# Attention of one transformer block: low value products one block later, merged steps, other filler rates

## The chip, the cores and the metric

The kernel runs on one core of one Trainium2 chip. The metric is the device time of one execution in microseconds, the median of several runs. Matrix products run on TensorE (PE in the profile, its weight loads PEld), elementwise work on VectorE (DVE), ScalarE (ACT) and GpSimd (POOL), and transfers are issued by SyncE (SP).

## What is computed

One transformer block over 512 positions with a model width of 1024, in float32. Cut to what matters here:

```python
proj = rmsnorm(x) @ w_in                       # queries, keys, values, gates
o_nsa = nsa_attention(...)                     # 8 heads, 2 key groups: compressed + selected + window
o_swa = swa_attention(...)                     # 8 heads, 2 key groups: window of 128, a sink per head
x = x + rmsnorm(concat([o_nsa, o_swa]) @ w_o)
x = x + rmsnorm((gelu(conv(h @ w_gate)) * (h @ w_up)) @ w_down)   # h = rmsnorm(x), 2816 wide
x = x + (p @ w_ple) * sigmoid(x @ w_ple_gate)
# inside each attention, per query block: s = q k^T * scale - slope * distance, masked;
# p = softmax(s) (SWA: with the sink in the denominator); o = p v
```

## The kernel before

Every float32 operand of a product is split into a high and a low part, and a product is three matmuls (high by high, low by high, high by low; `mm3`, L129) of up to 512 columns. The stages come in order: load and normalise, value projection, compressed keys, the first query projections, the attention, output projection, feed-forward, gate.

The attention goes by 16 units, a unit being one key group and one block of 128 queries (in the order 3, 0, 2, 1): eight NSA units (two groups), then eight SWA units. A unit has two parts, each a Python generator that issues a step's instructions and then yields a number of nanoseconds:

- Scores. `nsa_scores` (L592) has two steps a head, eight in all: score matmuls, bias and minimum on VectorE (L611), exponentials on ScalarE (L615), scaling by gate over sum on GpSimd (L521). `swa_scores` (L551) has four steps with the scores of a head each (L565, L567), and a fifth with the small operations, the exponentials (L578) and the scaling (L584).
- Value products. `pv` (L523) goes over the key blocks of a unit: four transposes of the probabilities into PSUM (L499), a copy of the high part on ScalarE (L501), the low part by subtraction on VectorE (L503), then two matmuls into one PSUM bank: the high product (L533) and the low product (L534). They come one block behind the transposes. After the last block `put_out` (L506) copies the sum out (L510, L515, L517, L518). The split tiles have three slots, the scores three PSUM banks, the transposes two and the sum one.

`together` (L664) merges the score steps of a unit with the product steps of the unit before it, so that both advance by equal fractions. After each step `fill` (L157) adds the step's nanoseconds times a rate (`RATES`, L55, for NSA group 0, 1, SWA group 0, 1) to a credit, and while the credit is positive it takes 650 off and issues one filler step. Fillers are work from elsewhere: the query and key projections that later units need (tiles 3, 8, 4, 5, 6, 7 in this order; nine steps each, eight of them one `mm3`), and, appended once unit 8's steps are out, the first half of the output projection (`out_proj_first`, L767; 33 steps, 32 of them three matmuls, L762 to L764), which reads the finished NSA outputs. What a unit needs is finished by `drain` ahead of it. What is left at the end is issued after the last unit.

The order on each engine is made by the compiler: it simulates the program with a time model and gives an engine the earliest instruction in program order that is ready. A filler's first matmul is also tied (`pin`, L139) behind an attention matmul, `self.last`, the last one issued before it; `att` (L178) keeps that. After the attention, `out_proj` (L780) computes the second half, and its matmuls of the later SWA group (`mixmm`, L757) need the last unit's output.

Of the kernel before, what the change touches and what calls it, by code (L numbers as in the profile page):

```python
# [14 lines left out]
P = 128  # L15
# [36 lines left out]

FILL_STEP = 650.0
WARM = 9
RATES = [0.5, 0.5, 0.7, 0.7]  # L55


class Block:
    def __init__(self, tc, io, ctx):
        self.tc = tc  # L60
        self.nc = tc.nc
        self.io = io
        en = ctx.enter_context
        self.cp = en(tc.tile_pool(name="const", bufs=1))
        self.up = en(tc.tile_pool(name="u", bufs=1))
        self.wrp = en(tc.tile_pool(name="wr", bufs=2))
        self.rp = en(tc.tile_pool(name="rb", bufs=2))
        self.sp = en(tc.tile_pool(name="s", bufs=4))
        self.tp = en(tc.tile_pool(name="tiny", bufs=2))
        self.pp = en(tc.tile_pool(name="ps", bufs=1, space=bass.MemoryType.PSUM))  # L70
        self.n = 0
        self.ordered = False
        self.e = []
        self.phase = "x"
        self.mark = {}
        self.fillers = []
        self.credit = 0.0
        self.rate = 1.0
        self.last = None
        self.pinned = None  # L80

    @contextmanager
# [74 lines left out]
    def fill(self, ns):  # L157

        self.credit += ns * self.rate
        while self.credit > 0 and self.fillers:  # L160
            self.credit -= FILL_STEP
            self.fill_step()

    def fill_step(self):
        phase, self.phase = self.phase, "fill"
        self.pinned = self.last
        try:
            next(self.fillers[0])
        except StopIteration:
            self.fillers.pop(0)  # L170
        self.pinned = None
        self.phase = phase
# [3 lines left out]
            self.fill_step()  # L176

    def att(self, r):  # L178
        self.last = r.ins
        return r  # L180


# [340 lines left out]
    def pv(self, blocks, mix, qt):  # L523

        nc = self.nc
        po = self.ps("o")
        n = len(blocks)

        def product(i, t, rows, v):
            if rows < P:  # L530
                self.att(nc.tensor.matmul(po, v, t[: 2 * rows, 0, :], start=i == 0, stop=i == n - 1))
                return
            self.att(nc.tensor.matmul(po, v, t[:, 0, :], start=i == 0, stop=False))  # L533
            self.att(nc.tensor.matmul(po, v, t[:, 1, :], start=False, stop=i == n - 1))  # L534

        late = None
        for i, (srcs, rows, v) in enumerate(blocks):
            t = self.transpose_split(srcs, rows)
            if late is not None:
                product(*late)  # L540
            late = (i, t, rows, v)
            yield 602
        product(*late)
        self.put_out(po, mix, qt)
        yield 1000

# [4 lines left out]
    def swa_scores(self, u):  # L551
        self.phase = "swa"
        nc = self.nc
        g, qt = u["g"], u["qt"]
        kh, kl = self.ks
        n = P if qt == 0 else 2 * P
        k0 = 0 if qt == 0 else (qt - 1) * P
        b0 = P if qt == 0 else 0
        p = self.u([P, 4, 2 * P], F32, "p")
        nm = self.tiny([P, 4], "nm")  # L560
        for r in range(4):
            if r % 2 == 0:
                ps = self.ps("s")
            o = ps[:, r % 2 * 256 : r % 2 * 256 + 256]
            self.score(ps, o, self.q[4 + 2 * g + r // 2][:, r % 2, qt * P : (qt + 1) * P],  # L565
                       kh[:, g, k0 : k0 + 256], kl[:, g, k0 : k0 + 256])
            nc.vector.tensor_tensor_reduce(p[:, r, :n], o[:, :n], self.dist_w[:, b0:], op0=ALU.add, op1=ALU.min,  # L567
                                           scale=SLOPES[4 * g + r], scalar=3e38, accum_out=nm[:, r : r + 1])
            yield 70 + n
        ns = self.nsink[:, 4 * g : 4 * g + 4]  # L570
        nm2 = self.tiny([P, 4], "nm2")
        nc.vector.tensor_tensor(nm2, nm, ns, op=ALU.min)
        es = self.tiny([P, 4], "es")
        nc.vector.tensor_sub(es, nm2, ns)
        nc.scalar.activation(es, es, AF.Exp)
        sm = self.tiny([P, 4], "sm")
        for r in range(4):
            nc.scalar.activation(p[:, r, :n], p[:, r, :n], AF.Exp, bias=nm2[:, r : r + 1], scale=-1.0,  # L578
                                 accum_out=sm[:, r : r + 1])
        rc = self.tiny([P, 4], "rc")  # L580
        nc.vector.tensor_add(rc, sm, es)
        nc.vector.reciprocal(rc, rc)
        for r in range(4):
            self.scale_rows(p[:, r, :n], rc[:, r : r + 1])  # L584
        yield 400
        u["blocks"] = [
            ([p[:, r, b * P : (b + 1) * P] for r in range(4)], P,
             self.vs[k0 // P + b][:, 4 + g].rearrange("p a d -> p (a d)"))
            for b in range(n // P)
        ]  # L590
# [70 lines left out]
    def mix_tiles(self):  # L661
        return [self.u([P, 2, T], F32R) for _ in range(2)]

    def together(self, a, b):  # L664

        gens = [(x, n) for x, n in (a, b) if x is not None]
        done = [0] * len(gens)
        alive = [True] * len(gens)
        while any(alive):
            k = min((k for k in range(len(gens)) if alive[k]), key=lambda k: (done[k] + 1) / gens[k][1])  # L670
            try:
                ns = next(gens[k][0])
                done[k] += 1
                self.fill(ns)
            except StopIteration:
                alive[k] = False

    def attention(self):
        io = self.io
# [2 lines left out]
        mix = [None] * 4  # L682
# [44 lines left out]
        units += [dict(kind="s", g=g, qt=qt) for g in range(2) for qt in (3, 0, 2, 1)]  # L727
        before = None
        for i, u in enumerate(units + [None]):
            sc = None  # L730
            if u is not None:
                k = u["g"] + (0 if u["kind"] == "n" else 2)
                need = [[], [2, 3], [8, 4, 5], [6, 7]][k]
                for f in need:
                    if f in qf:
                        self.drain(qf[f])
                if mix[k] is None:
                    mix[k] = self.mix_tiles()
                self.rate = RATES[k]
                u["mix"] = mix[k]  # L740
                sc = (self.nsa_scores(u), 8) if u["kind"] == "n" else (self.swa_scores(u), 5)
            bp = None
            if before is not None:
                bp = (self.pv(before["blocks"], before["mix"], before["qt"]), len(before["blocks"]) + 1)
            self.together(sc or (None, 1), bp or (None, 1))
            if i == NQT * 2:
                self.mix = []
                for k in range(2):
                    self.mix += [(mix[k][0][:, i, :], mix[k][1][:, i, :]) for i in range(2)]
                self.fillers.append(self.out_proj_first())  # L750
            before = u
# [264 lines left out]
```

## Time and profile before

| | us |
|---|---|
| three runs | 690.43, 691.87, 692.05 |
| their median | 691.87 |
| the profiled execution, device time | 691.2 |
| its span, first to last instruction | 689.4 |
| TensorE busy in the span | 665.5 |

The profile is one execution. A busy matmul row says little of how close together matmuls start, since each one's modelled end lies past the start of the next. The attention runs from about 75 to 236 us of the span.

### The profile page before, as it was taken

Reading aid. Unit: us, or ns where it says so; the run is one execution under the profiler, and the core shown is the slowest. Engines: PE = TensorE matmul, PEld = TensorE weight load, DVE = VectorE, ACT = ScalarE, POOL = GpSimd, SP = SyncE. Lnnn points to the kernel's source line nnn. Section 1 sums busy time; section 2 is a strip of 40 time slices with the busy share of each in tenths; the row PEclk is TensorE's granted clock in tenths of the full one; section 3 lists DMA queues with packets and bytes.
Section 4 is the critical chain, followed back from the end, with each engine's and each line's share of the span. In section 5 each row is a group of like instructions: output and inputs, shape, how many; then the busy total and the mean of one; then the engine's idle time right before and its main releaser. Section 6 shows DMA issues by size and latency. Waiting matters only on the chain.

```text
span 689.4 us, 8840 instructions
## 1 busy us (share of the span) xinstructions
PE 665.5 (97%) x3111; PEld 545.1 (79%) x3111; DVE 399.9 (58%) x808; ACT 324.9 (47%) x603; POOL 170.4 (25%) x235
## 2 busy tenths in 40 slices
PE   8999999999979897999999999999999999999996
PEld 7988777887758685888888888888888888887785
DVE  6786767767964468767555455554542232325853
ACT  7453758867796455445333343333432222233341
POOL 1112658757375152422010110101100000100000
PEclk9999999999999999999999999999999999999999
DMA  8537523111106143042233322233323323344032
GB/s 290 178 99 222 145 62 78 46 47 48 47 1 214 38 162 121 15 140 92 92 101 109 97 91 92 92 99 116 92 85 86 105 85 101 97 145 152 2 106 77
DMA packets 25116, 70.05 MB, mean 102 GB/s; under 512 B 3184, under 2 KB 4464, under 8 KB 25072
## 3 DMA queue, kind: packets, MB, share of 16 engines
q1 hardware_dynamic: 24928, 69.42, 32.1%
q8 instruction: 24, 0.39, 0.2%
q14 instruction: 20, 0.16, 0.1%
q10 hardware_dynamic: 144, 0.08, 0.0%
HBM read 60.05 MB, written 2.10 MB: 90 GB/s over the span
## 4 chain that ended last, share of the span: by engine, by line
PE 87%; DVE 5%; ACT 5%; DMA 1%; issue 1%; POOL 0%; ACTq 0%; DVEq 0%
PE mlpup_pss L136 4%; PE mlpup_pss L137 4%; PE mlpup_pss L133 4%; PE mlpup_psmm L136 3%; PE mlpup_psmm L133 3%; PE mlpup_psmm L137 3%; PE mlpup_pst L136 3%; PE mlpup_pst L137 3%; PE mlpup_pst L133 3%; PE nsa_pst L499 3%; PE mlpdown_pss L133 2%; PE mlpdown_pss L137 2%; PE mlpdown_pss L136 2%; ACT swa_u L578 2%; PE fill_psmm L133 2%; PE fill_psmm L136 2%
## 5 line engine op out<-in xcount | busy, mean ns | idle before, releaser
L117 ACT ACTIVATE mlpup_wh<-mlpup_wr 128x1024 fp32r<-128x1024 f32 x40 | 42.3, 1060 | 83.3 <-PE mlpup_pss L136 27.7
L870 POOL TENSOR_TENSOR mlpup_s<-mlpup_s,r3b 128x512 f32<-128x512 f32 x22 | 29.3, 1332 | 188.0 <-ACT mlpup_s L869 188.0
L117 ACT ACTIVATE mlpdown_wh<-mlpdown_wr 128x1024 fp32r<-128x1024 f32 (+1 forms) x24 | 23.7, 989 | 84.7 <-PE mlpdown_pss L136 33.9
L121 DVE TENSOR_TENSOR mlpdown_wh<-mlpdown_wr,mlpdown_wh 128x1024 fp32r<-128x1024 f32 (+1 forms) x24 | 27.3, 1136 | 62.2 <-ACT mlpdown_wh L117 62.2
L121 DVE TENSOR_TENSOR mlpup_wh<-mlpup_wr,mlpup_wh 128x1024 fp32r<-128x1024 f32 x40 | 49.4, 1236 | 10.6 <-ACT mlpup_wh L117 10.5
L136 PE MATMUL mlpup_pss<-r_u,mlpup_wh 128*128 128x512 f32 x120 | 46.8, 390 | 0.2 <-DVE mlpup_wh L121 0.2
L133 PE MATMUL mlpup_pss<-r_u,mlpup_wh 128*128 128x512 f32 x120 | 46.8, 390 | 0.0
L137 PE MATMUL mlpup_pss<-r_u,mlpup_wh 128*128 128x512 f32 x120 | 46.7, 389 | 0.0
L521 POOL TENSOR_SCALAR nsa_u<-nsa_u,nsa_nrc,gate 128x512 f32<-128x512 f32 (+3 forms) x64 | 38.3, 609 | 26.8 <-DVE nsa_nrc L646 19.2
L615 ACT ACTIVATE nsa_u<-nsa_u,nsa_nnm 128x512 f32<-128x512 f32 (+3 forms) x64 | 35.4, 555 | 7.1 <-DVE nsa_nnm L611 6.5
L503 DVE TENSOR_TENSOR nsa_u<-nsa_pst,nsa_u 128x512 fp32r<-128x512 f32 (+1 forms) x44 | 30.0, 688 | 14.9 <-ACT nsa_u L501 14.6
L611 DVE CUSTOM_DVE_ANT_0 nsa_u<-nsa_pss,biastables_u 128x512 f32<-128x512 f32 (+3 forms) x64 | 30.2, 486 | 6.6 <-PE nsa_pss L549 6.4
L501 ACT ACTIVATE nsa_u<-nsa_pst 128x512 fp32r<-128x512 f32 (+1 forms) x44 | 25.5, 589 | 15.8 <-PE nsa_pst L499 15.6
L221 POOL TENSOR_TENSOR mlpdown_s<-mlpdown_s,mlpdown_s 128x512 f32<-128x512 f32 x6 | 7.8, 1296 | 100.2 <-ACT mlpdown_s L220 100.2
L869 ACT ACTIVATE mlpup_s<-mlpup_s 128x512 f32<-128x512 f32 x22 | 13.8, 631 | 38.6 <-DVE mlpup_s L868 38.6
L121 POOL TENSOR_TENSOR fill_wh<-fill_wr,fill_wh 128x512 fp32r<-128x512 f32 (+1 forms) x14 | 24.7, 1761 | 28.7 <-ACT fill_wh L117 28.7
L133 PE MATMUL mlpup_pst<-r_u,mlpup_wh 128*128 128x512 f32 x80 | 31.2, 390 | 0.0
L137 PE MATMUL mlpup_pst<-r_u,mlpup_wh 128*128 128x512 f32 x80 | 31.1, 389 | 0.0
L136 PE MATMUL mlpup_pst<-r_u,mlpup_wh 128*128 128x512 f32 x80 | 31.1, 389 | 0.0
L133 PE MATMUL mlpup_psmm<-r_u,mlpup_wh 128*128 128x512 f32 x80 | 31.1, 389 | 0.0
L136 PE MATMUL mlpup_psmm<-r_u,mlpup_wh 128*128 128x512 f32 x80 | 31.1, 389 | 0.0
L137 PE MATMUL mlpup_psmm<-r_u,mlpup_wh 128*128 128x512 f32 x80 | 31.1, 389 | 0.0
(396 smaller groups left out, 1941.7 us busy)
## 6 DMA issues: line engine op xcount, KB each, us to landing
mlpup_wr<-in_gu_dram SPq DMA_DIRECT2D x40, 512.0 KB, 3.3
mlpdown_wr<-in_down_dram SPq DMA_DIRECT2D x16, 512.0 KB, 3.6
fill_wr<-in_win_dram SPq DMA_DIRECT2D x6, 512.0 KB, 3.5
mlpdown_wr<-in_down_dram SPq DMA_DIRECT2D x8, 384.0 KB, 3.2
fill_u<-fill_u SPq DMA_DIRECT2D x20, 128.0 KB, 2.3
loadx_u<-in_xT_dram SPq DMA_DIRECT2D x8, 256.0 KB, 4.8
compress_u<-projk_u SPq DMA_DIRECT2D x16, 128.0 KB, 2.3
fill_wr<-in_wo_dram SPq DMA_DIRECT2D x8, 256.0 KB, 3.0
```

The lines of the kernel that those rows point to most:

```text
L117: nc.scalar.activation(hi, raw, AF.Copy)
L121: eng.tensor_sub(lw, raw, hi.bitcast(F32))
L133: r = self.pin(mm(ps, hi, x[:, 0, :], start=start, stop=False))
L136: mm(ps, lo, x[:, 0, :], start=False, stop=False)
L137: mm(ps, hi, x[:, 1, :], start=False, stop=stop)
L499: self.att(nc.tensor.transpose(pt[:rows, r * P : (r + 1) * P], src, self.ident))
L501: nc.scalar.activation(t[:rows, 0, :], pt[:rows], AF.Copy)
L503: nc.vector.tensor_sub(lo, pt[:rows], t[:rows, 0, :].bitcast(F32))
L521: self.nc.gpsimd.tensor_scalar(ap, ap, col, gate, op0=ALU.mult, op1=ALU.mult)
L611: nc.vector.tensor_tensor_reduce(dst, src, dist, op0=ALU.add, op1=ALU.min, scale=SLOPES[8 + 4 * g + r], scalar=3e38, accum_out=nm[:, r, b ...
L615: nc.scalar.activation(dst, dst, AF.Exp, bias=nm[:, r, b : b + 1], scale=-1.0, accum_out=sm[:, r, b : b + 1])
L870: nc.gpsimd.tensor_mul(c0, c0, self.r3)
```

## The change

Four edits. In `pv` the high product still comes one block behind the transposes, and the low product now two blocks behind. `together` takes a list of keys for each generator, one for each step, and always advances the generator whose next key is least: NSA scores have (j + 1) / 8, products 0.2 + (j + 1) / n, and SWA scores four zeros and a 2.0, so that an SWA unit's first four steps come first, then the products of the unit before it, then the step with the exponentials. A filler is tied to the last attention matmul of six steps back (`LAG`) in place of the last one. The rates go from 0.5, 0.5, 0.7, 0.7 to 0.36, 0.36, 0.9, 0.6, and SWA score steps yield 100, 100, 100 and 4 n + 380 in place of 70 + n each.

```diff
-RATES = [0.5, 0.5, 0.7, 0.7]
+RATES = [0.36, 0.36, 0.9, 0.6]
+LAG = 6
...
-        self.last = None
+        self.steps = [None]
...
         self.credit += ns * self.rate
+        self.steps.append(self.steps[-1])
         while self.credit > 0 and self.fillers:
...
-        self.pinned = self.last
+        self.pinned = self.steps[max(0, len(self.steps) - 1 - LAG)]
...
     def att(self, r):
-        self.last = r.ins
+        self.steps[-1] = r.ins
         return r
...
-        def product(i, t, rows, v):
-            if rows < P:
-                self.att(nc.tensor.matmul(po, v, t[: 2 * rows, 0, :], start=i == 0, stop=i == n - 1))
-                return
-            self.att(nc.tensor.matmul(po, v, t[:, 0, :], start=i == 0, stop=False))
-            self.att(nc.tensor.matmul(po, v, t[:, 1, :], start=False, stop=i == n - 1))
-
-        late = None
+        def product(i, part, start, stop):
+            t, rows, v = ts[i]
+            rhs = t[: 2 * rows, 0, :] if rows < P else t[:, part, :]
+            self.att(nc.tensor.matmul(po, v, rhs, start=start, stop=stop))
+
+        ts = []
         for i, (srcs, rows, v) in enumerate(blocks):
-            t = self.transpose_split(srcs, rows)
-            if late is not None:
-                product(*late)
-            late = (i, t, rows, v)
+            ts.append((self.transpose_split(srcs, rows), rows, v))
+            if i > 0:
+                product(i - 1, 0, i == 1, False)
+            if i > 1:
+                product(i - 2, 1, False, False)
             yield 602
-        product(*late)
+        last = blocks[-1][1] == P
+        product(n - 1, 0, n == 1, False)
+        if n > 1:
+            product(n - 2, 1, False, not last)
+        if last:
+            product(n - 1, 1, False, True)
         self.put_out(po, mix, qt)
         yield 1000
...
-            yield 70 + n
+            yield 100 if r < 3 else 4 * n + 380
...
-    def together(self, a, b):
-
-        gens = [(x, n) for x, n in (a, b) if x is not None]
-        done = [0] * len(gens)
-        alive = [True] * len(gens)
-        while any(alive):
-            k = min((k for k in range(len(gens)) if alive[k]), key=lambda k: (done[k] + 1) / gens[k][1])
+    def together(self, *gens):
+
+        left = [(g, list(keys)) for g, keys in gens]
+        while left:
+            k = min(range(len(left)), key=lambda k: left[k][1][0] if left[k][1] else 0.0)
             try:
-                ns = next(gens[k][0])
-                done[k] += 1
+                ns = next(left[k][0])
+                left[k][1].pop(0)
                 self.fill(ns)
             except StopIteration:
-                alive[k] = False
+                left.pop(k)
...
-                sc = (self.nsa_scores(u), 8) if u["kind"] == "n" else (self.swa_scores(u), 5)
-            bp = None
+                if u["kind"] == "n":
+                    gens.append((self.nsa_scores(u), [(j + 1) / 8 for j in range(8)]))
+                else:
+                    gens.append((self.swa_scores(u), [0.0, 0.0, 0.0, 0.0, 2.0]))
             if before is not None:
-                bp = (self.pv(before["blocks"], before["mix"], before["qt"]), len(before["blocks"]) + 1)
-            self.together(sc or (None, 1), bp or (None, 1))
+                n = len(before["blocks"]) + 1
+                gens.append((self.pv(before["blocks"], before["mix"], before["qt"]), [0.2 + (j + 1) / n for j in range(n)]))
+            self.together(*gens)
```

## Rows read from the trace of the kernel before

**Rows 1.** The page: span, and busy time, share and instructions by engine.
```profile
span 689.4 us, 8840 instructions
...
PE 665.5 (97%) x3111; PEld 545.1 (79%) x3111; DVE 399.9 (58%) x808; ACT 324.9 (47%) x603; POOL 170.4 (25%) x235
```

**Rows 2.** Windows by stage: stretch, its length, busy us by engine, granted clock, DMA.
```profile
76.00:181.00 105.00, 103.24 (x567) 83.00 (x566) 77.52 (x305) 77.44 (x212) 68.73 (x110) 1.00 0.25 65
181.00:205.00 24.00, 19.56 (x112) 15.07 (x111) 19.56 (x93) 21.99 (x81) 14.23 (x32) 1.00 0.01 2
205.00:234.00 29.00, 27.84 (x134) 22.33 (x132) 13.12 (x24) 18.41 (x36) 12.55 (x15) 1.00 0.43 145
234.00:242.00 8.00, 6.09 (x18) 4.55 (x19) 3.41 (x6) 3.32 (x6) 0.81 (x2) 0.79 0.10 33
310.00:600.00 290.00, 290.00 (x1279) 239.78 (x1278) 136.62 (x161) 99.49 (x120) 31.36 (x24) 1.00 0.31 95
```

**Rows 3.** TensorE's waits, 76 to 250 us: who waits for whom, total, times, longest.
```profile
PE outproj_psmm L762 <- ACT swa_u L517: 2.1, 1, 2.1
PE swa_pso L533 <- DVE swa_s L515: 1.6, 2, 0.9
...
PE fill_psmm L762 <- ACT fill_u L778: 1.0, 1, 1.0
PE nsa_pso L534 <- DVE nsa_u L503: 0.9, 4, 0.2
PE fill_psmm L763 <- POOL nsa_u L518: 0.9, 1, 0.9
```

**Rows 4.** Windows of the filler matmuls alone: stretch, length, TensorE's busy us, clock, DMA.
```profile
76.00:181.00 105.00, 42.01 (x150) 1.00 0.25 65
181.00:198.00 17.00, 0.00 (x0) 1.00 0.01 2
...
205.00:234.00 29.00, 17.68 (x72) 1.00 0.43 145
```

**Rows 5.** The chain of waits, 181 to 205 us: shares by engine and line.
```profile
by line: ACT swa_u L578 40.0%; ACT swa_u L501 10.7%; DVE swa_u L567 7.7%; DVE swa_u L503 7.6%; issue 6.9%; DVE nsa_s L515 3.5%; DVE swa_nm L572 3.1%; ACT swa_s L510 2.7%; ACT swa_es L575 2.6%; ACT nsa_s L510 2.5%; ACT fill_wh L117 2.2%; PE 
```

**Rows 6.** TensorE's timeline from 89 us: start, duration, instruction, idle before it.
```profile
89.19 0.49 PE L533 MATMUL nsa_pso<-nsa_u,vnatural_u 128*128 128x512 f32 x1
89.92 0.50 PE L534 MATMUL nsa_pso<-nsa_u,vnatural_u 128*128 128x512 f32 x1 [0.23 <-DVE nsa_u L503]
```

**Rows 7.** Groups of ScalarE, VectorE, GpSimd, 181 to 234 us: busy, mean ns, idle before.
```profile
L578 ACT ACTIVATE swa_u<-swa_u,swa_nm 128x256 f32<-128x256 f32 (+1 forms) x28 | 13.0, 467 | 0.0
L501 ACT ACTIVATE swa_u<-swa_pst 128x512 fp32r<-128x512 f32 (+1 forms) x18 | 10.4, 591 | 2.1 <-PE swa_pst L499 1.9
...
L510 ACT ACTIVATE swa_s<-swa_pso 64x512 f32<-64x512 f32 x8 | 4.8, 594 | 3.0 <-PE swa_pso L534 2.9
...
L503 DVE TENSOR_TENSOR swa_u<-swa_pst,swa_u 128x512 fp32r<-128x512 f32 (+1 forms) x18 | 12.3, 686 | 8.5 <-ACT swa_u L501 8.4
...
L515 DVE TENSOR_TENSOR swa_s<-swa_pso,swa_s 64x256 f32<-64x256 f32 x14 | 5.8, 417 | 7.5 <-ACT swa_s L510 4.9 <-ACT swa_es L575 1.8 <-POOL nsa_u L518 0.8
...
L521 POOL TENSOR_SCALAR swa_u<-swa_u,swa_rc 128x256 f32<-128x256 f32 (+1 forms) x32 | 13.9, 451 | 12.8 <-DVE swa_nm L567 4.6 <-ACT swa_u L578 3.4 <-ACT swa_es L575 2.1
```

**Rows 8.** TensorE's timeline at the tail: the stop ahead of the out-projection.
```profile
235.83 0.73 PE L762 MATMUL outproj_psmm<-swa_u,outproj_wh 128*128 128x512 f32 x2 [2.14 <-ACT swa_u L517]
```

**Rows 9.** The chain, 205 to 250 us: start, time to the next piece, what.
```profile
223.04 0.87 PE swa_pst L499 x8
...
228.23 0.24 PE fill_psmm L762
...
238.31 0.43 PE outproj_psmm L763
```

**Rows 10.** From a query projection to its use: GpSimd's group, then SP's timeline (issue, landing).
```profile
L373 POOL TENSOR_TENSOR fill_u<-fill_s,fill_u 128x512 fp32r<-128x512 f32 x6 | 7.8, 1296 | 0.0
...
111.76 2.38 SPq L228 DMA_DIRECT2D projq_u<-fill_u  x4
```

More of the change, by code (lines that the diff above doesn't have):

```diff
@@ L729, in attention @@
         for i, u in enumerate(units + [None]):
-            sc = None
+            gens = []
             if u is not None:
```

## The prediction

> **What bounds the kernel now.** The first look is at the page: TensorE is busy 97% of 689.4 us, no other engine over 58% [rows 1]. So the time is TensorE's work plus the time in which it stands, and this change adds and removes no matmul. All it can win or lose is standing time, so the second view is the windows by stage [rows 2]. The last row, the feed-forward part, is the yardstick: nothing ends a wait there, and the weight loads, one ahead of each matmul, are busy 239.78 of 290 us, or 0.827. A busy matmul row hides standing time, since the modelled end of one matmul reaches past the start of the next; the share of weight loads hides less. Dividing each stage's weight loads by 0.827 gives the time it would need at that pace:
> - 76 to 181 us, the NSA units (selected and window attention): 83.00 / 0.827 = 100.4 of 105, so 4.6 lost.
> - 181 to 205, the "hole": 15.07 / 0.827 = 18.2 of 24, 5.8 lost.
> - 205 to 234, SWA units (sliding window with sink) with fillers: 27.0 of 29, 2.0 lost.
> - 234 to 242, the tail: 5.5 of 8, 2.5 lost, and the granted clock is 0.79.
>
> [...] By matmul busy time the four losses would be 1.8, 4.4, 1.2 and 1.9, 9.3 in all instead of 14.9.
>
> The waits then say what stood [rows 3]. The longest is the tail: the first out-projection matmul that needs the last SWA output waits 2.1 us for ScalarE [rows 3, 8]. [...] The hole has a plain cause in the windows of the filler matmuls [rows 4]: from 181 to 198 there is none. The input-projection fillers (tiles 3, 8, 4 to 7) are used up at the end of the NSA units, and the out-projection fillers need the last NSA output, which is stored only after unit 8's value products. In the hole the chain of waits lies on ScalarE, 40% of it in the SWA exponentials [rows 5], and ScalarE is busy 22.0 of 24 us [rows 2]. [...]
>
> **The change part by part.** The sum is made against the profiled execution's 691.2 us; the median of the three runs, 691.87, is 0.7 above it.
>
> Fillers moved. A step adds its nanoseconds times the rate to a credit, and 650 buy one filler step. Units 0 to 7 yield 8 x (752 + 368 + 624 + 496) per group for scores and 24 x 602 + 4 x 1000 for value products; two groups, less the last unit's products (4010, run in unit 8), make 68.7 thousand. At 0.5 that buys 53 steps, at 0.36 it buys 39 (the first is free). A projection tile takes nine steps, eight of them three matmuls of 0.227 us. So 48 triples run in the NSA units before and 35 after: 13 x 0.68 = 8.9 us of filler leave them. Tile 6's last six steps and tile 7 now fall into SWA units 8 to 10, where the hole is, and the out-projection fillers start in unit 10, when their input has long been stored. In units 8 to 15 the new rates buy 39 steps, and two more in the tail; of the 33 out-projection steps 7 are left when everything is emitted, against none before.
>
> Hole: 5.8 us lost, with work for it on hand. ScalarE is next in line there: the softmax of a unit takes four exponentials of 0.467, the copies behind the transposes 0.591 each, the output copy 0.594 [rows 7], some 4 us a unit and the small ones, against 2.7 of attention matmuls (eight transposes 0.87, four products 0.92, eight half-wide scores 0.91) and some 4 us (unit rate 0.9) or 2.7 us (0.6) of filler. TensorE has the longer share, but not by much in the last four units. I take 4.9 of 5.8, ends 0 and 5.8; and in the units up to the tail 0.5 of 2.0, ends 1.0 lost and 2.0 won.
>
> Tail: from the last exponentials to the output 4 x 0.467 + 4 x 0.451 (GpSimd scaling) + 0.591 + 0.686 + 0.594 + 2 x 0.417 = 6.4 us [rows 7], and two transposed blocks and a last copy between, some 8. [...] I take 3.6 of 4.1, ends 0 and 4.1.
>
> Low products one block later. Four times in the NSA units the low product starts 0.73 us after the high one where 0.23 is the pace, because VectorE's subtraction ends late: 0.50 each [rows 3, 6]. Later by a block, it has four transposes (0.44) and a high product (0.23) more ahead of it [rows 9], 0.67 us. So 4 x 0.50 = 2.0 could go; I take 1.8, ends 0 and 2.3. No matmul or weight load is added. What the delay adds is a wait: a split tile (three slots) lives a block longer, and ScalarE's copy of block i+1 needs the slot of block i-2, whose low product is issued just ahead of block i+1's transposes, for which the copy waits anyway. The exponentials are queued behind that copy; the cover goes only if the compiler puts the transposes ahead of the low product, at 0.23 a block.
>
> NSA units with less filler. VectorE and ScalarE are each busy 77.5 of 105 us there [rows 2], some 76 after the move. TensorE goes from 100.4 to about 91.5 us of work. So it stays the longest, the next engine at 83% of it where it was 77%, but units 2 and 6 (384-wide scores over a three-block product) have little cover left. With score steps 0.2 of a unit ahead of the products, and fillers that may be taken six steps early, some of it is made good. The price lies between nothing and the whole 8.9 us (a stage that stays as long as it was, paced by VectorE); nearer to the yardstick than to the hole, which had no filler at all, I take 1.5.
>
> Tile 5 now ends within unit 7, and unit 8's third score needs it: beside VectorE and ScalarE steps there is GpSimd's 1.3 us and a 2.38 us transfer [rows 10]. Between them lie the rest of unit 7 and unit 8's first scores, some 7 us of TensorE work; nothing taken, at worst 2 us. The SP queue sees the same transfers, in the same order, later.
>
> Sum: -4.9 - 0.5 - 3.6 - 1.8 + 1.5 = -9.3, so 691.2 - 9.3 = 681.9 us, or 682.6 against the median; I say 682.5.
>
> **The rivals.**
> - The NSA units give it back. The moved filler is missed there, at half to the full 8.9 us: 691.2 - 10.8 + 4.5 to 8.9 = 685 to 689, and with a hole only half filled up to 692. For it: VectorE and ScalarE are close to TensorE in single units. Against it: TensorE has 15 us more work than either over the stage.
> [...]
> - Slower, by the SWA softmax. The step with a unit's exponentials (L570 to L585) is now put behind all products of the unit before, and the unit's own products come after only four heads' scores of the next (0.91 us) and two filler steps (1.4). The chain in between is 4 x 0.467 + 4 x 0.451 + the small ones, 4.4 us [rows 7], so some 2.1 us stand open in each of 7 units, 14.7 in all, if no filler from further on fills it. Against today's 5.8 + 2.0 that is 6.9 more, and if the remaining steps are spent on it the tail wins nothing: 691 + 6.9 - 1.8 + 1.5 = 698. It decides at 7.8 / 7 = 1.1 us a unit. Against it: six steps' freedom puts three or four filler steps within reach.
> [...]
> - Nothing happens: the queue's order is the compiler's, not the program's, and if its own time model already sees TensorE busy everywhere, lag and keys change little: 691.
>
> **How the numbers follow.** Forecast (679 to 686.5) 0.46; given back (686.5 to 692.5) 0.20; all of it (674 to 679) 0.14; nothing (690 to 693) 0.07; softmax chain 0.10; clock 0.03. A measurement can tell about 0.3%, 2.1 us, from no change: faster is below 689.8, slower above 694. Faster: 0.46 + 0.14 + 0.12 of the given-back case = 0.72. Same: the rest of that case and most of "nothing", 0.14. Slower: 0.14. The range 675 to 692.5 leaves out the slower cases and the lower edge of "all of it", about 0.19.
>
> **What would show it.** In the profile after, filler matmuls between 175 and 200 us and no wait of out-projection on the store of NSA's last output; no 2 us wait ahead of the out-projection and a granted clock of 1.00 there; waits of the low product on VectorE gone; the weight-load share of the NSA stage not below 0.79. I am wrong if TensorE's waits on VectorE's score steps or on ScalarE's exponentials in the NSA or SWA units grow by more than 5 us together, or if the tail still waits.

## The result, and the profile after

The changed kernel takes 686.93 us (median of four runs, 685.68 to 687.33) against 691.70 of the kernel before (four runs, 690.43 to 692.05): a ratio of 0.9931, interval 0.9913 to 0.9950. The gain is 4.8 us; 9.3 were forecast. The profiled execution after took 687.33 us, 3.9 less than the profiled one of before. Line numbers have moved: L501 transposes, L503 and L505 split (before L499, L501, L503), L534 is both products, L573 the minimum of SWA's scores (L567), L584 its exponentials (L578), L769 to L771 the output projection (L762 to L764).

The page after, where TensorE is busy as long as before [rows 1], and the windows by stage that answer to [rows 2] (the columns as there; the third row is a new stretch, and the tail now ends at 252):

```profile
span 685.4 us, 8840 instructions
...
PE 666.0 (97%) x3111; PEld 546.6 (80%) x3111; DVE 400.1 (58%) x808; ACT 325.2 (47%) x603; POOL 170.8 (25%) x235
```

```profile
76.00:181.00 105.00, 101.74 (x565) 80.29 (x563) 82.78 (x332) 82.15 (x231) 70.18 (x117) 1.00 0.22 59
181.00:205.00 24.00, 24.00 (x124) 20.07 (x124) 11.85 (x40) 16.93 (x44) 13.16 (x18) 1.00 0.27 82
205.00:217.00 12.00, 9.79 (x40) 7.51 (x39) 8.85 (x38) 10.04 (x35) 8.91 (x18) 0.72 0.47 157
217.00:230.00 13.00, 13.00 (x67) 10.91 (x66) 6.86 (x13) 9.02 (x18) 3.67 (x4) 1.00 0.20 70
230.00:252.00 22.00, 22.00 (x98) 18.07 (x97) 12.80 (x19) 11.22 (x18) 8.31 (x7) 1.00 0.44 144
```

The hole is closed: from 181 to 205 us the weight loads are busy 20.07 us where they were 15.07, which by the yardstick 0.827 is the whole stretch. From 217 to 252 nothing is lost, the tail included, and the clock is 1.00. Two rows go the other way. The NSA units have 80.29 us of weight loads where they had 83.00, and between 205 and 217 TensorE stands and the granted clock is 0.72; before, that place was covered with fillers.

The filler matmuls alone (stretch, length, TensorE's busy us, clock, DMA), beside [rows 4], and TensorE's waits from 76 to 250 us, beside [rows 3]:

```profile
76.00:181.00 105.00, 31.15 (x114) 1.00 0.22 59
181.00:198.00 17.00, 11.71 (x48) 1.00 0.21 63
198.00:205.00 7.00, 5.43 (x21) 1.00 0.41 127
205.00:214.00 9.00, 0.03 (x1) 0.76 0.46 160
214.00:234.00 20.00, 11.93 (x45) 0.94 0.25 81
```

```profile
PE swa_pss L554 <- DVE swa_nm L573: 1.3, 2, 1.1
PE swa_pso L534 <- ACT swa_u L503: 0.9, 1, 0.9
PE nsa_pss L554 <- DVE nsa_nnm L617: 0.8, 2, 0.6
PE swa_pss L554 <- DMA fill_u<-fill_u: 0.7, 2, 0.5
PE nsa_pso L534 <- ACT nsa_u L503: 0.6, 2, 0.4
PE swa_pst L501 <- DVE swa_u L505: 0.5, 1, 0.5
PE swa_pso L534 <- DVE swa_u L505: 0.2, 1, 0.2
```

The fillers left the NSA units as counted (150 records fell to 114, 12 triples) and stand in the old hole, 48 of them where there was none. The out-projection's wait of 2.1 us is gone, and so are the four waits of the NSA low product. New are the two waits at the top. TensorE's timeline shows where they lie (start, duration, instruction, idle before it):

```profile
204.46 0.39 PE L771 MATMUL fill_psmm<-nsa_u,fill_wh 128*128 128x512 f32 x1
...
206.53 0.28 PE L555 MATMUL swa_pss<-projq_u,fill_u 128*128 128x256 f32 x1
207.90 0.39 PE L554 MATMUL swa_pss<-projq_u,fill_u 128*128 128x256 f32 x1 [1.09 <-DVE swa_nm L573]
...
211.77 1.70 PE L534 MATMUL swa_pso<-swa_u,vnatural_u 128*128 128x512 f32 x3 [0.94 <-ACT swa_u L503]
...
214.97 0.63 PE L771 MATMUL fill_psmm<-projq_u,fill_wh 128*128 128x512 f32 x1
215.40 0.63 PE L534 MATMUL swa_pso<-swa_u,vnatural_u 128*128 128x512 f32 x1
215.83 0.63 PE L769 MATMUL fill_psmm<-projq_u,fill_wh 128*128 128x512 f32 x1
```

Up to 209.59 the lines, most of them left out, are the scores of nine heads, more than two units in one run, with four transposes and no filler among them. Behind the one at 206.53 TensorE stands until VectorE has read a score bank. Then the products of an earlier unit stand 0.94 us for ScalarE's copy. From 209.6 to 216.4 us the granted clock is 0.50, so it fell behind the first stop, and the second lies within it: matmuls there start 0.43 us apart where they had come 0.23 apart. By the sum over starts below, 3.9 of the 6.4 us lost from 205 to 217 lie in these 6.8 us, the second stop (1.3) included. ScalarE's timeline says why the copy is late:

```profile
209.06 0.51 ACT L584 ACTIVATE swa_u<-swa_u,swa_nm 128x256 f32<-128x256 f32 x1 [0.37 <-DVE swa_nm L578]
...
210.55 0.50 ACT L584 ACTIVATE swa_u<-swa_u,swa_nm 128x256 f32<-128x256 f32 x1
...
211.14 1.06 ACT L503 ACTIVATE swa_u<-swa_pst 128x512 fp32r<-128x512 f32 x2
```

ScalarE worked almost without a pause from 202.8 us on (7.9 of 8.3 us up to the copy), and had four exponentials of one unit (two of them shown) ahead of the copy that TensorE waited for.

**Where the time went, in one table.** Lost time can also be read from the starts: the time from one matmul's start to the next, less the pace seen when they follow directly (0.227 us for 512 columns, 0.119 for the 256 of an SWA score, 0.109 for a transpose, 0.429 for the product of the compressed keys). By that sum over the profiled executions:

| stretch, us | lost before | lost after | change | forecast |
|---|---|---|---|---|
| 70 to 76, entry | 1.6 | 0.3 | -1.3 | 0 |
| 76 to 181, NSA units | 8.8 | 12.0 | +3.2 | -0.3 (-1.8 + 1.5) |
| 181 to 205, hole | 8.2 | 0.4 | -7.8 | -4.9 |
| 205 to the tail, SWA units | 1.7 | 6.5 | +4.8 | -0.5 |
| the tail | 4.4 | 0.0 | -4.4 | -3.6 |
| together | 24.7 | 19.2 | -5.5 | -9.3 |

The tail's 4.4 before are the stop ahead of the out-projection and slower starts behind it. The chain of before (start, time to the next piece), and its windows of TensorE alone (stretch, length, busy, clock, DMA), show those:

```profile
237.37 0.23 PE outproj_psmm L762
...
237.89 0.43 PE outproj_psmm L764
...
240.45 0.43 PE outproj_psmm L762
```

```profile
235.00:240.00 5.00, 4.09 (x12) 0.76 0.00 0
240.00:245.00 5.00, 5.00 (x22) 0.90 0.31 105
```

The last matmul of the output projection indeed starts 5.4 us earlier (256.7 to 251.3); 1.4 us of that are lost again behind it, which is told at the end. The rows go by fixed times, and the work in them has moved: the last product of the compressed keys, which ends the NSA units, stands at 190.5 us before and at 180.8 after. Counted by units, entry and NSA units lost 13.2 before and 12.3 after, the SWA units up to the tail 7.1 and 6.9. So what was won behind 190 was lost again at 206, and the SWA units as a whole won next to nothing. By the weight-load yardstick the NSA row is 4.6 and 7.9, the same +3.3. In the row from 205 it shows only 2.9 lost of 12 between 205 and 217 (12 less 7.51 / 0.827), where the starts show 6.4: 5.6 us of work at full pace would have 4.6 us of weight loads, and there are 7.51. A load ahead of a 512-column matmul lasts 331 ns there, where the granted clock is 0.50, against 188 from 217 to 230 at 1.00, so the weight-load yardstick hides half of what was lost here, and this text goes by the sum over starts.

### The profile page after: what moved, and what is told of

It reads as the page before. It is cut to its first block, busy times and chain, and to the rows that moved or that the text cites. A ratio compares the mean times of both kernels' runs of the same rounds, so it can differ in the third digit from the quotient of the medians.

```text
span 685.4 us, 8840 instructions
## 1 busy us (share of the span) xinstructions
PE 666.0 (97%) x3111; PEld 546.6 (80%) x3111; DVE 400.1 (58%) x808; ACT 325.2 (47%) x603; POOL 170.8 (25%) x235
## 4 chain that ended last, share of the span: by engine, by line
PE 86%; DVE 5%; ACT 3%; DMA 2%; POOL 1%; issue 1%; SPq 0%; ACTq 0%; POOLq 0%; DVEq 0%
PE mlpup_pss L138 5%; PE mlpup_pss L137 5%; PE mlpup_pss L134 4%; PE mlpup_psmm L137 3%; PE mlpup_psmm L134 3%; PE mlpup_psmm L138 3%; PE nsa_pso L534 3%; PE mlpup_pst L138 3%; PE mlpup_pst L134 3%; PE mlpup_pst L137 3%; PE mlpdown_pss L134 2%; PE mlpdown_pss L138 2%; PE mlpdown_pss L137 2%; PE nsa_pst L501 2%; PE mlpdown_pst L138 1%; PE mlpdown_psmm L138 1%
## 5 line engine op out<-in xcount | busy, mean ns | idle before, releaser
L505 DVE TENSOR_TENSOR nsa_u<-nsa_pst,nsa_u 128x512 fp32r<-128x512 f32 (+1 forms) x43 | 29.0, 684 | 9.1 <-ACT nsa_u L503 8.8
L122 POOL TENSOR_TENSOR fill_wh<-fill_wr,fill_wh 128x512 fp32r<-128x512 f32 (+1 forms) x14 | 24.7, 1767 | 33.9 <-ACT fill_wh L118 33.9
L503 ACT ACTIVATE nsa_u<-nsa_pst 128x512 fp32r<-128x512 f32 (+1 forms) x43 | 25.1, 592 | 13.4 <-PE nsa_pst L501 13.1
```

The source lines that it names most:

```text
L122: eng.tensor_sub(lw, raw, hi.bitcast(F32))
L503: nc.scalar.activation(t[:rows, 0, :], pt[:rows], AF.Copy)
L505: nc.vector.tensor_sub(lo, pt[:rows], t[:rows, 0, :].bitcast(F32))
```

## The experiments

Two theories stood against each other at first. By **supply** the gain comes from the rates: work is kept for the hole and the tail, and the tie matters little. By **freedom** the gain comes from the tie six steps back, which lets a filler in while the latest attention matmul still waits. Each run is measured beside the kernel before on the same chip. The chips differ between rows, and the kernel before took 691.70 to 692.50 us on them, so medians of two rows compare to about 1 us.

| kernel | median us | ratio to before | interval |
|---|---|---|---|
| after | 686.93 | 0.9931 | 0.9913 to 0.9950 |
| after, old rates | 688.48 | 0.9951 | 0.9929 to 0.9974 |
| after, tie to the last matmul | 690.79 | 0.9985 | 0.9961 to 1.0008 |
| after, low product one block behind | 689.13 | 0.9966 | 0.9944 to 0.9988 |
| after, old merging and yields | 685.57 | 0.9908 | 0.9876 to 0.9939 |
| before, new rates alone | 698.69 | 1.0108 | 1.0077 to 1.0139 |
| before, tie six back alone | 688.48 | 0.9950 | 0.9931 to 0.9969 |
| before, low product late alone | 690.86 | 0.9983 | 0.9965 to 1.0001 |
| before, low late and tie six back | 690.33 | 0.9987 | 0.9969 to 1.0005 |
| the same, rates part of the way | 690.26 | 0.9984 | 0.9964 to 1.0005 |
| after, tie twelve back | 688.89 | 0.9959 | 0.9945 to 0.9974 |
| after, tie twelve back, the rest kept for the tail | 688.86 | 0.9964 | 0.9946 to 0.9982 |
| after, tie 24 back | 695.41 | 1.0059 | 1.0036 to 1.0082 |

**Each part undone.** The rates first.

```diff
-RATES = [0.36, 0.36, 0.9, 0.6]
+RATES = [0.5, 0.5, 0.7, 0.7]
```

> The changed kernel with the rates of before (0.5, 0.5, 0.7, 0.7), all else changed. By the supply theory (what counts is that filler lies where TensorE stands) the hole without filler behind the NSA units and the stop ahead of the out-projection come back, since no out-projection step is left at the end: 690 to 693 us. By the freedom theory (the ties and the order of steps let the compiler fill stops with what there is) most of the gain stays: 686 to 688.

Measured 688.48 us, between the two: 3.6 us are still gained beside the kernel before on its chip (692.07), and the tail's wait is back, since nothing is left for it:

```profile
PE outproj_psmm L769 <- ACT swa_u L519: 2.1, 1, 2.1
PE swa_pso L534 <- DVE swa_s L517: 2.1, 1, 2.1
```

So what the rates do for the tail is shown, and the rest of the gain has another source. The hole does not come back, as supply had it: by starts 2.4 us are lost there, against 8.2 before. Next the tie.

```diff
-LAG = 6
+LAG = 0
```

> The changed kernel with fillers tied to the last attention matmul (lag 0), all else changed. By the supply theory a filler lies in its unit anyway, and this is worth up to 1.5 us: 686.5 to 688.5. By the freedom theory stops open all over, as many as the six steps filled: 690 to 694.

Measured 690.79 us: of 4.8 us only about 1 is left, and its interval reaches no change, as freedom said. TensorE's wait for ScalarE's copies in the SWA units is 2.3 us in one piece, with fillers on hand, and the tail is as closed as in the change.

```diff
-            if i > 0:
-                product(i - 1, 0, i == 1, False)
-            if i > 1:
-                product(i - 2, 1, False, False)
+            if late is not None:
+                product(*late)
+            late = (i, t, rows, v)
```

> The changed kernel with low value products one block behind, as before. By the prediction's term of 1.8 us, and with less filler between blocks to hide the subtraction: 688.5 to 690, with stops of 0.5 us between high and low products on VectorE in the NSA units. If the delay is worth nothing: 686 to 687.5.

Here `product` issues the high and the low product of a block together. Measured 689.13 us, 2.2 above the change; the intervals overlap a little, so the size is rough. The waits that the prediction named are back:

```profile
PE nsa_pso L536 <- DVE nsa_u L505: 1.6, 7, 0.2
```

There are seven in the NSA units, each with the low product 0.50 us behind its pace, as in [rows 6].

```diff
-            k = min(range(len(left)), key=lambda k: left[k][1][0] if left[k][1] else 0.0)
+            k = min((k for k in range(len(gens)) if alive[k]), key=lambda k: (done[k] + 1) / gens[k][1])
...
-            yield 100 if r < 3 else 4 * n + 380
+            yield 70 + n
```

> The changed kernel with steps merged by fractions as before and the old yields of SWA score steps, all else changed (10 out-projection steps are left at the end instead of 7). If the new stop in the last SWA units comes from the late exponentials, it goes, and the time is 683 to 686. If the lead of 0.2 and the order of SWA steps help, 687 to 690.

Measured 685.57 us (684.94 to 686.01), the fastest median of all runs. The interval overlaps that of the change, so that merging by keys costs 1.4 us is likely and not settled; a gain from it is not seen. Its windows (columns as in the windows by stage):

```profile
181.00:205.00 24.00, 22.89 (x121) 18.57 (x120) 15.56 (x51) 17.15 (x46) 13.61 (x21) 1.00 0.28 78
205.00:217.00 12.00, 10.35 (x56) 7.92 (x55) 8.04 (x33) 11.90 (x42) 8.95 (x19) 1.00 0.36 110
```

The clock stays at 1.00 in the stretch where the change has 0.72, no wait of TensorE from 76 to 250 us is longer than 0.6 us, and the losses by starts there are 3.4 instead of 6.4 us (with 2.1 more in the hole). The other traces point the same way. From 205 to 234 us, the tail's stop left out, the kernels merged by keys lose 3.4 to 7.0 us (9.1 with the tie 24 back), those merged by fractions 1.3 to 3.5 (9.6 with the new rates alone), in one execution each. The merge alone on the kernel before was not run, and the run above changes merge and yields together. The kernel with the old merging beats both others by its median; against the change the runs don't decide.

**Each part alone.** The rates on the kernel before (the diff above, turned round), and the tie alone:

> The kernel before with the new rates alone. By the supply theory (prediction: hole -4.9, tail -3.6, NSA units +1.5 and 1.8 more, since the low products aren't delayed) it wins 5 to 8 us: 684 to 687. By the freedom theory (leave-one-out has given the tie 3.8 us and the rates 1.6) fillers tied to the last matmul can't fill what the thinner NSA units open: 690 to 693, with the tail's stop gone and new waits on VectorE in the NSA units.

> The kernel before with fillers tied six steps back alone. By the supply theory the hole keeps its cause (no filler at all from 181 to 198 us) and the tail too: 690 to 692, and if fillers are spent earlier, up to 694. By the freedom theory it wins about what its absence cost the changed kernel, 3 to 4 us: 687 to 689.

The rates alone make the kernel 7 us slower, 698.69, which neither theory had; the tie alone gives 3.6 us where the whole change gives 4.8, as freedom expected. The rates' profile, 5 us windows of TensorE alone (busy, clock, DMA), and its waits:

```profile
215.00:220.00 5.00, 2.20 (x9) 1.00 0.00 0
220.00:225.00 5.00, 4.94 (x19) 0.66 0.88 281
```

```profile
PE swa_pso L533 <- ACT swa_u L501: 2.6, 3, 1.9
PE swa_pso L533 <- DVE swa_s L515: 2.2, 2, 1.6
PE nsa_pso L531 <- DVE swa_u L503: 1.9, 1, 1.9
PE nsa_pso L533 <- ACT nsa_u L501: 1.8, 2, 1.5
PE nsa_pso L534 <- DVE nsa_u L503: 1.6, 7, 0.2
```

TensorE stands 2.8 of 5 us at 215 with out-projection fillers unissued, which come right behind, 0.43 us apart, in the window with a clock of 0.66. By starts the NSA stretch loses 16.4 us (8.8 before), 1.8 of them from 161.9 to 165.4, where the granted clock is low (0.98 in the mean from 76 to 187), and the stretch from 205 to 234 loses 9.6 (4.0 before, the tail's stop of 2.3 included). With fewer fillers in the NSA units more of the waits there lie open, and in the SWA units a filler that is tied to the newest attention matmul stands behind the very matmul that waits. That the tie is the reason is an inference from this run beside the one with all but the tie changed (690.79 against 686.93); that tie and rates work only together is measured: on top of tie and late low product the new rates give 4.8 us (690.33 to 685.57), without either they cost 7.

The tie alone wins in the hole: by starts 3.2 us are lost there instead of 8.2, and 1.6 less at the entry. Its two stretches, 76 to 181 and the hole (columns as in the windows by stage):

```profile
76.00:181.00 105.00, 100.24 (x551) 81.03 (x550) 78.01 (x309) 76.91 (x210) 68.81 (x110) 0.98 0.23 63
181.00:205.00 24.00, 22.92 (x130) 18.44 (x129) 19.56 (x88) 23.02 (x81) 14.97 (x32) 1.00 0.06 19
```

The wait that stays with the tie alone is the tail's, as with the old rates above:

```profile
PE outproj_psmm L764 <- ACT swa_u L519: 2.1, 1, 2.1
```

The low product alone, and both together:

> The kernel before with low products a block later alone. By the prediction's term four stops of 0.5 us go: 1.8 us, 689.5 to 690.5. If the delay only pays where blocks follow each other without filler (in the changed kernel it was worth 2.2), or if its third live tile makes new waits: 691 to 693.

> The kernel before with the tie six steps back and the delayed low products, rates and merging as before. If the two add (3.6 and about 2): 685.5 to 687. The tail's stop should still be there, as nothing is left for it. If the rates are what the tie needs: 688 to 689.

The low product alone gives some 1.2 to 1.6 us, near the forecast 1.8, though its interval reaches no change. Both together give 690.33, not the sum of 3.6 and 1.4 but less than the tie alone; the intervals of tie alone and both meet at 0.9969. Parts of this change don't add. Each edit makes the compiler place the whole attention anew, and which of the other small waits come up is not foreseen. The runs leave one candidate: the mean granted clock of an execution is 0.992 in the median with both, 0.997 with the tie alone and 0.996 with the low product alone. By an estimate from these numbers, 0.0045 of 688 us, that is some 3 us, about what the sum lacks. The kernel with the new rates beside both (685.57) has 0.997 again. Why these two don't add, and why the clock is lower with both, stays open.

**How far back, and how much filler.** Would more freedom close what is left?

```diff
-LAG = 6
+LAG = 12
```

> The changed kernel with the tie twelve steps back. If the new stop in the last SWA units (206 to 212 us, no filler matmul from 204.5 to 214) stands because the fillers on hand are tied behind products that wait for ScalarE, it is filled and its low clock goes: 682 to 684.5. If the fillers are late because their weights are split late on ScalarE and GpSimd, the stop stays: 686 to 688.

> The changed kernel with the tie 24 steps back, three to four SWA units. If more freedom is always better, as with 12 or a little under: 682 to 684. If fillers are then spent early in the NSA units and are missed behind them, the hole and the tail's stop come back: 688 to 692.

No: 688.89 and 695.41 us (for 24 the same edit with 24). With twelve the low clock between 209 and 217 is gone (the mean of the profiled execution is 0.996, in the change 0.992), and from 205 to 234 us 3.8 us are lost besides the tail's stop, where the change loses 6.5; but the tail's stop of 2.3 us is back, with 1.6 lost at the low clock behind it. TensorE's waits, first with twelve, then with 24:

```profile
PE swa_pso L534 <- DVE swa_s L517: 2.2, 2, 1.5
PE outproj_psmm L769 <- ACT swa_u L519: 2.1, 1, 2.1
```

```profile
PE swa_pso L534 <- DVE swa_s L517: 4.1, 2, 2.9
PE nsa_pst L501 <- POOL nsa_u L523: 2.6, 1, 2.6
PE swa_pso L534 <- DVE swa_u L505: 2.5, 2, 1.4
```

With twelve steps 141 filler matmuls are done by 180 us, with six 126: the freedom is spent early, and the tail has nothing left. With 24 the longest waits are those of attention matmuls. To see whether the tail alone explains twelve, the leftover steps were tied to the last unit's second product step:

```diff
+        self.steps += [self.steps[-3]] * (LAG + 1)
         while self.fillers:
             self.fill_step()
```

> The changed kernel with the tie twelve steps back, but the out-projection steps left at the end tied to the last unit's second product step. If twelve steps lost against six because the fillers kept for the tail were spent early (the 2.3 us stop and its low clock came back), the stop closes and it wins 4 us against that run: 684 to 685.5. If the loss lies in the units before, it stays at 687.5 to 689.

The tail's wait goes away, and the time stays, 688.86 us: the first line of the waits is now

```profile
PE swa_pso L534 <- DVE swa_s L517: 3.8, 3, 1.7
```

so 1.6 us more are waited in the SWA units for what was kept for the tail. The stop moved with the filler.

**Milder rates**, on the kernel before with tie and late low product:

```diff
-RATES = [0.5, 0.5, 0.7, 0.7]
+RATES = [0.42, 0.42, 0.8, 0.55]
```

> As the run before, with rates 0.42, 0.42, 0.8, 0.55, a step between the old and the new: NSA units keep 45 filler steps (before 53, changed 39), 8 out-projection steps are left at the end. If filler is to be spread, thick enough for the NSA units and with some for the tail: 682.5 to 685, below the run with the changed rates and old merging (685.6). If these rates matter no more: 685 to 687.

690.26 us, no better than with the old rates (690.33), where the full step gives 685.57. Its NSA stretch loses 14.7 us by starts, 10.8 with the old rates and 10.4 with the new ones without the merging; but 3.4 of the 14.7 lie in a stretch at a lower clock (112.4 to 119.2 us, in this execution, whose mean is 0.993), and without it the three are near each other. So by the medians the time doesn't go evenly with the rates, and the best ones can't be worked out from the amount of filler alone; where the 4.7 us between the two lie is not shown.

## Why the prediction was right or wrong

**The side was right, the sum was twice too large.** The step that failed is the term of the SWA units from 205 us on: it was taken at -0.5, with the merged steps at no cost, and measured +4.8. Together with the hole, and counted by units, the SWA units were to win 5.4 us and won 0.2. The forecast's own bounds, 679 to 686.5, miss 686.93; the outer range, 675 to 692.5, holds it because it is wide and takes in no change at all.

- *Hole* (-4.9): right. By the yardstick all 5.8 went, by starts 7.8; counted from the last product of the NSA units on, it is 5.0. Fillers stand between 175 and 200, and nothing waits for the store of NSA's output, as asked for under what would show it. That the rates closed it, as the term has it, is not shown: the tie alone does most of it too, and with the old rates and all else changed it stays closed.
- *Tail* (-3.6): right, 4.4 by starts; no wait is left, and the clock there is 1.00. No row or run shows the 4.1 that the term was taken out of; in its place the trace of before shows a wait of 2.1 us, then starts 0.43 us apart, 4.4 lost together. Every run with the old rates has the 2.1 us again, and so has the tie twelve back.
- *Low products* (-1.8): right by mechanism and about by size: 2.2 when undone, 1.2 to 1.6 alone, with intervals as wide as that.
- *Thinner NSA* (+1.5, bounds 0 to 8.9): somewhat too small. The weight-load share of 76 to 181 is 80.29 / 105 = 0.765, under the 0.79 given as the mark. The stretch lost 3.2 more instead of 0.3 less, so the price there is 5.0 if the low products gave their 1.8. Half of that is only a matter of place, since more of units 7 and 8 now runs before 181. Counted from 70 us to the last product of the compressed keys, 13.2 were lost before and 12.3 after; with 1.3 won at the entry and some 2 at the low products, the price is 2.4. The kernel before only just met the mark of 0.79 (83.00 / 105). The prediction divided a stage of 105 us by its mean load, TensorE 91 us against 76, and took that margin for cover; the waits that are left come in single units, on VectorE's score steps and ScalarE's copies. With the rates alone most of the upper bound 8.9 was paid: 7.6 us by starts in the NSA stretch, 1.8 of them where the granted clock is low.
- *SWA units from 205* (-0.5, ends -2.0 and +1.0): wrong, +4.8 and outside its ends. The rival that had the mechanism was the SWA softmax: scores first, exponentials late. Its place was right (VectorE's score steps, then ScalarE's exponentials ahead of a copy), its price not: it reckoned with 2.1 us open in each of seven units, and it happened in one place, at 206.5 to 212, with a clock of 0.50 from 209.6 to 216.4. With the old merging the clock doesn't fall there and the whole is 685.57. That the merge is the cause fits the profiles; the times alone don't settle it.
- *The clock in the NSA units* (a slower kernel, chance 0.03): not borne out in the kernel after. The granted clock is 1.00 from 76 to 181 with 31 us of filler where there were 42; behind that it was 0.50 from 209.6 to 216.4 and from 264.2 to 267.6, where TensorE had waited before, 1.1 and 1.4 us. But the case was not idle: in the profiled executions of four neighbours the clock did fall in the NSA units, at 162 us with the rates alone (0.98 from 76 to 187), at 90 with the tie alone (0.98 from 76 to 181), at 112 with the milder rates (0.993 over the execution) and at 91 with the tie 24 back (0.987 over the execution), each time behind starts 1.5 to 2.7 us late, and that cost 1.5 to 3.4 us.
- *The tie* had no term of its own, only a clause as cover in two places. It is the largest of the parts measured alone: 3.6 us. Without it the rest of the change gives about 1 us, not clear of nothing, and the new rates by themselves lose 7. So the forecast gain rested on a mechanism that it didn't price, and that the side came out right is in part luck.
- *Entry* (no term): 1.3 won, since with fillers tied further back some came into a stop at 70 to 76 us; every kernel with the tie six or more back has less than 0.8 lost there, each with the newest matmul as tie 1.5 or more.
- *Behind the out-projection* (no term): 1.4 lost again.
- *Tile 5 in time for unit 8* (nothing, at worst 2): right, one wait of 0.5 us for the transfer, at 158 us, and one of 0.2 later.

The rival "given back" (685 to 692) has the number and not the place: the hole and the tail were won in full, but by units the NSA units gave back some 2 us and the stretch from 205 on 4.8. For the place the softmax rival came nearer.

## What to carry to other kernels

When independent work is moved by rates between stages on one engine, price first what may pass what: the amount of filler in a stage only bounds the gain, and its ties decide whether it can be there when the engine would stand. Then look at single units rather than stage means: here 4.8 us were lost in one place, around the scores of nine heads that came without a filler among them. Where work moves, count losses by units too, since fixed windows of time put part of one stage's loss to the next. And measure parts together as well as one by one: here the rates lost 7 us alone and gave 5 on top of the tie and the late low product.

## What the hardware showed that was not expected

The granted clock fell after like stops in one execution and not in another. TensorE alone in the normalisation stage, first after, then before (stretch, length, busy, clock, DMA):

```profile
260.00:265.00 5.00, 3.06 (x11) 0.92 0.46 149
265.00:270.00 5.00, 5.00 (x18) 0.74 0.00 0
```

```profile
265.00:270.00 5.00, 3.15 (x13) 1.00 0.50 167
270.00:275.00 5.00, 4.94 (x22) 1.00 0.00 0
```

The stops ahead of the first feed-forward matmul were 1.38 us in the one and 1.30 in the other, with the same work around them; in the kernel after the matmuls behind it start 0.43 us apart for 3 us, in the kernel before 0.23. Seven such starts cost 7 x 0.20 = 1.4 us, what was lost again. The same shows over many executions of one program: of 26 of the kernel before on one chip, the eight with a mean granted clock of 0.998 took 689.5 to 690.0 us, and the others, at 0.997 to 0.992, 691.0 to 694.3. A single execution of this kernel therefore says little about 3 us, and the stage sums above, which come from one execution each, are uncertain by as much; the kernel with both the tie and the late low product was profiled at 692.9 us, 2.6 above its median.
